# Hybrid block on one core: gates, attention output, GLU, merge and output projection with tokens on the partitions

## The chip, the cores and the metric

One core of a Trainium2 chip runs the whole kernel. Its engines are PE (matrix products and transposes), DVE and ACT (element work, conversions, copies), POOL (element work, a little of it here) and SP, whose queue issues the weight loads. Each runs its own instructions in order, and semaphores tie them together. The metric is the device time of one execution in microseconds; the median of three runs is given.

## The reference, cut to what matters

There are 256 tokens of width 1024, all in float32.

```python
h = rms_norm(x, norm_mix_g)
q, k, v, u, g = split(h @ w_in)              # 1024, 1024, 1024, 512, 2048 columns
o_a = attention(rotary(q), rotary(k), v)     # 8 heads of 128, causal, one block of 256
y   = gelu(ssm(u))                           # 512 channels
val, gt = split(y @ w_glu)                   # 1024 columns each
o_b = val * sigmoid(gt)
g_a, g_b = split(g)
mixed = sigmoid(g_a) * o_a + sigmoid(g_b) * o_b
x = x + mixed @ w_out
h = rms_norm(x, norm_mlp_g)
x = x + square(relu(h @ w_up)) @ w_down      # 4096 columns between
out = rms_norm(x, norm_final_g)
```

## The kernel before

Each float32 product is made of three products of parts: weights and activations are split into a high part in the format that PE takes at speed and a low part, and `mm3` (lines 85 to 88) issues high by high, high by low and low by high. Weights come in units of 128 partitions by 1024 numbers, 512 KB each. A unit is loaded by SP into one of five `raw` buffers, ACT casts it to `hi` (line 82), and DVE subtracts to get `lo` (line 83). There are four `hi` and four `lo` buffers, so a cast waits until PE has finished with the unit four before it.

Most projections keep channels on the partitions and tokens on the free axis: a 128x128 piece of the weights is stationary and 256 columns of activations stream against it. Values `v` (`v_chunk`) and the down projection have it the other way round: a 128x128 piece of the activations is stationary, 512 columns of weights stream, and the result has tokens on the partitions. The gates (`gate`) use `proj_pair`, two units at a time; the accumulated result is multiplied by the norm's factor `rs_bc`, laid along the free axis (line 317), and goes through a tanh on ACT. `attn_out` turns the probabilities on PE (`pt`, line 298), copies them out on ACT (`pts`, line 300), multiplies by `v` into `o`, and joins the gate `tha` to it. The GLU (lines 595 to 611) reads the SSM's output after a gelu, `yhl`, split in high and low, and merges with the second gate `thb` into `mxh` and `mxl`. The output projection (lines 618 to 633) adds the residual and leaves `x2h` and `x2l` for the up projection. `tok_major` (line 658) later turns the residual stream to token layout for the down projection.

The norm's factor per token is made by POOL in a short chain of small operations (`rsqrt`, lines 179 to 182) and then laid along the free axis by PE (`rs_ps`, line 196).

What comes after what is set in two steps. The string `ORDER` names the parts in program order: V the values, K a pair of heads' q and k, S scores and softmax, G and A the first gate and the attention output, B the second gate, Q and T the SSM, X a load of ACT's function table, Y the gelu. From the program order and the dependencies a scheduler then decides each engine's own order when the program is built. The splits of weights have a high priority there.

Of the kernel before, what the change touches and what calls it, by code (L numbers as in the profile page):

```python
# [13 lines left out]
ALU = mybir.AluOpType  # L14
# [29 lines left out]
ORDER = ("V0 V1 P0 T0 C0 Q0 T1 Q1 T2 K0 T3 X0 S0 G0 A0 G1 K1 K2 S1 Q2 A1 K3 G2 S2 A2 Q3 "  # L44
         "B0 B1 G3 S3 X1 Y0 A3 B2 B3")


def build(ctx, tc, dr, out):
# [151 lines left out]
    rs_bc = rs.unsqueeze(1).to_broadcast([P, 2, T])  # L200
# [42 lines left out]

    def v_chunk(c):
        acc = [mm_bank(f"v{c}{h}").rearrange("p a b -> p (a b)") for h in range(2)]
        for kk_ in range(4):
            wh, wl = in_unit(4 * c + kk_, "v")
            for k2 in range(2):
                k = 2 * kk_ + k2
                w2h, w2l = wh[:, k2 * 512 : (k2 + 1) * 512], wl[:, k2 * 512 : (k2 + 1) * 512]  # L250
                for hf in range(2):
                    xh, xl = xgh[:, k, hf * P : (hf + 1) * P], xgl[:, k, hf * P : (hf + 1) * P]
                    PE.matmul(acc[hf], xh, w2h, start=(k == 0), stop=False)
                    PE.matmul(acc[hf], xh, w2l, start=False, stop=False)
                    PE.matmul(acc[hf], xl, w2h, start=False, stop=(k == KD - 1))
# [15 lines left out]
    mixA = p1.tile([P, KD, T], F32, name="mixA")  # L271
# [31 lines left out]
    def attn_out(hp, prs, tha):  # L303
        pts = [attn_pt(x) for x in prs]
        o = att_bank("o")
        for j in range(2):
            hd = 2 * hp + j
            PE.matmul(o[:, j, :], v[:, 0, hd * P : (hd + 1) * P], pts[j][:, 0:256],
                      start=True, stop=False, skip_group_check=True)
            PE.matmul(o[:, j, 128:256], v[:, 1, hd * P : (hd + 1) * P], pts[j][:, 256:384],  # L310
                      start=False, stop=True, skip_group_check=True)
        V.scalar_tensor_tensor(mixA[:, 2 * hp : 2 * hp + 2, :], tha, 1.0, o,
                               op0=ALU.add, op1=ALU.mult)

    def gate(first, dst):
        acc = proj_pair(first, "g")
        V.tensor_mul(dst, acc, rs_bc)
        act(dst, dst, AF.Tanh, scale=0.5)

    def prepare():  # L320
# [82 lines left out]
        def cmul(o_r, o_i, x_r, x_i, y_r, y_i, neg_i):  # L403
            # (x_r + i x_i)(y_r + i y_i); with neg_i, x_i and o_i stand for minus their parts
# [146 lines left out]
    yhl = []  # L551

    def gelu():
        yhl.append(p1.tile([P, KD, T], F32R, tag="yhl", name="yhl"))
        yflat = yT.rearrange("p m e j -> p m (e j)")
        for m in range(4):
            act(yflat[:, m, :], yflat[:, m, :], AF.Gelu_apprx_tanh)
            split(yhl[0][:, m, :], yhl[0][:, 4 + m, :], yflat[:, m, :])

    thb, qk, prs, tha = [None] * 4, {}, {}, {}  # L560
    for step in ORDER.split():
# [12 lines left out]
        elif part == "K":  # L574
            qk[n] = (rope(proj_pair(8 + 6 * n, "q"), "q"), rope(proj_pair(10 + 6 * n, "k"), "k"))
# [3 lines left out]
        elif part == "G":  # L579
            tha[n] = p1.tile([P, 2, T], F32, tag="tha", bufs=2, name="tha")  # L580
            gate(12 + 6 * n, tha[n])
        elif part == "A":
            attn_out(n, prs.pop(n), tha.pop(n))
        elif part == "Y":
            gelu()
        elif part == "Q":
            ssm_quad(n)
        elif part == "B":
            thb[n] = p1.tile([P, 2, T], F32, tag=("cs", "sn")[n // 2], bufs=4, name=f"thb{n}")
            gate(32 + 2 * n, thb[n])  # L590

# [1 line left out]
    mxh = keep.tile([P, KD, T], F32R, tag="b40", name="mxh")  # L593
    mxl = keep.tile([P, KD, T], F32R, tag="b41", name="mxl")
    for m in range(KD):
        wh, wl = w_unit(dr["w_glu"][m], f"glu{m}")
        acc = mm_bank(f"glu{m}")
        for j in (1, 0):
            for k in range(4):
                o = (2 * k + j) * P  # L600
                mm3(acc[:, j, :], wh[:, o : o + P], wl[:, o : o + P],
                    yhl[0][:, k, :], yhl[0][:, 4 + k, :], k == 0, k == 3)
        sg = p1.tile([P, T], F32, tag="sg", bufs=2, name="sg")
        act(sg, acc[:, 1, :], AF.Tanh, scale=0.5)
        V.scalar_tensor_tensor(sg, sg, 1.0, acc[:, 0, :], op0=ALU.add, op1=ALU.mult)
        tb = thb[m // 2][:, m % 2, :]
        V.scalar_tensor_tensor(tb, tb, 1.0,
                               sg.rearrange("p (e j) -> p j e", e=2), op0=ALU.add, op1=ALU.mult)
        V.scalar_tensor_tensor(mixA[:, m, :], tb, 0.5, mixA[:, m, :],
                               op0=ALU.mult, op1=ALU.add)  # L610
        split(mxh[:, m, :], mxl[:, m, :], mixA[:, m, :])
    ph1.__exit__(None, None, None)

# [1 line left out]
    p2 = ctx.enter_context(tc.tile_pool(name="ph2", bufs=1))  # L615
    xT = p2.tile([P, KD, T], F32, name="xT2")
    nc.sync.dma_start(xT, dr["xT"])
    accs = [mm_bank(f"wo{i}") for i in range(3)] + [bank("y", 1, "wo3")]
    for k in range(KD):
        wh, wl = w_unit(dr["w_out"][k], f"wo{k}")  # L620
        for m in range(KD):
            mm3(accs[m // 2][:, m % 2, :], wh[:, m * P : (m + 1) * P], wl[:, m * P : (m + 1) * P],
                mxh[:, k, :], mxl[:, k, :], k == 0 and m % 2 == 0, k == KD - 1,
                skip_group_check=True)
    x2h = keep.tile([P, KD, T], F32R, tag="xh", name="x2h")
    x2l = keep.tile([P, KD, T], F32R, tag="xl", name="x2l")
    for i in range(4):
        xc = xT[:, 2 * i : 2 * i + 2, :]
        V.scalar_tensor_tensor(xc, accs[i], 0.5, xc, op0=ALU.mult, op1=ALU.add)  # L629
        for m in (2 * i, 2 * i + 1):  # L630
            S.activation(x2h[:, m, :], xT[:, m, :], AF.Copy, scale=g_mlp[:, m : m + 1])
            V.scalar_tensor_tensor(x2l[:, m, :], xT[:, m, :], g_mlp[:, m : m + 1],  # L632
                                   x2h[:, m, :].bitcast(F32), op0=ALU.mult, op1=ALU.subtract)

# [19 lines left out]
    x2t = p2.tile([P, 2, D], F32, name="x2t")  # L654
    sq2 = p2.tile([P, D], F32, name="sq2")
    st2 = p2.tile([P, 16], F32, name="st2")

    def tok_major():
        for hf in range(2):
            for c in range(2):  # L660
                tp = att_bank("tp").rearrange("p a b -> p (a b)")
                for i in range(4):
                    PE.transpose(tp[:, i * P : (i + 1) * P],
                                 xT[:, 4 * c + i, hf * P : (hf + 1) * P], ident)
                S.copy(x2t[:, hf, c * 512 : (c + 1) * 512], tp)
# [85 lines left out]
def _layout(inp):  # L751
# [16 lines left out]
    parts.append(seg["gb"].reshape(8, P, 1024))
# [61 lines left out]
```

## Time and profile before

| what | value |
|---|---|
| runs | 407.99, 406.92, 407.28 us; median 407.28 us |
| profiled execution | span 406.2 us; no other time of its own is given |
| PE busy | 395.7 us of the span (97%) |
| DVE busy | 295.0 us (73%) |
| ACT busy | 229.2 us (56%) |
| POOL busy | 33.8 us (8%) |
| DMA | 71.62 MB, mean 176 GB/s |

The span runs from the first to the last instruction that the profiler has of one execution. Matmuls overlap each other in the rows, so the distance between the starts of two neighbours, not the length of one, is what a matmul adds to PE's time. The granted clock of PE is given as a share of full speed; 1.00 is the level of 2.4 GHz and 0.50 that of 1.2 GHz.

### The profile page before, as it was taken

How to read it: one execution, taken by the hardware profiler on the slowest of the kernel's cores; microseconds unless marked ns; L12 is line 12 of the kernel's file. 1: busy time of each engine (PE TensorE's matmuls, PEld its weight loads, DVE VectorE, ACT ScalarE, POOL GpSimd, SP SyncE). 2: the span in 40 equal slices, each digit the busy share in tenths (PEclk: the TensorE clock that was granted, in tenths of full speed). 3: DMA queues.
4: the chain of work that ended last, by engine and by line, in shares of the span. 5: the costliest groups of instructions: out<-in, count | busy, mean ns of one | idle time of the engine just before them, and what ended most of it. 6: DMA issues, size and time to landing. Idle time of an engine off the chain costs nothing.

```text
span 406.2 us, 7401 instructions
## 1 busy us (share of the span) xinstructions
PE 395.7 (97%) x2907; PEld 369.5 (91%) x2907; DVE 295.0 (73%) x530; ACT 229.2 (56%) x363; POOL 33.8 (8%) x39
## 2 busy tenths in 40 slices
PE   7989999999999999999999999999999999999993
PEld 4968999999899998999999999999999888899983
DVE  6999899998998996769657656666666544563424
ACT  6878777464374565945637764545455344344323
POOL 4392562000000000000000000000000000000000
PEclk8999999999999999999999999999999999999998
DMA  7986843255526254366684365656565655565202
GB/s 223 390 326 189 264 146 99 89 188 171 162 63 207 73 163 141 111 195 215 186 330 160 119 215 185 194 171 197 169 197 168 203 194 181 195 207 166 94 0 105
DMA packets 22786, 71.62 MB, mean 176 GB/s; under 512 B 2784, under 2 KB 4832, under 8 KB 22624
## 3 DMA queue, kind: packets, MB, share of 16 engines
q1 hardware_dynamic: 20016, 69.18, 52.3%
q10 hardware_dynamic: 2736, 1.97, 1.6%
q8 instruction: 23, 0.38, 0.4%
q14 instruction: 11, 0.09, 0.1%
HBM read 69.18 MB, written 1.05 MB: 173 GB/s over the span
## 4 chain that ended last, share of the span: by engine, by line
PE 91%; DVE 3%; POOL 2%; issue 1%; DMA 1%; ACT 1%; SPq 0%; DVEq 0%
PE up L87 8%; PE up L86 8%; PE up L88 8%; PE dn L685 5%; PE dn L686 5%; PE dn L687 5%; PE g L86 4%; PE g L87 4%; PE g L88 4%; PE q L86 2%; PE k L87 2%; PE k L88 2%; PE q L87 2%; PE glu L88 2%; PE glu L87 2%; PE glu L86 2%
## 5 line engine op out<-in xcount | busy, mean ns | idle before, releaser
L86 PE MATMUL up<-x2h,hi_up 128*128 128x256 f32 x256 | 72.6, 284 | 0.1
L87 PE MATMUL up<-x2l,hi_up 128*128 128x256 f32 x256 | 72.7, 284 | 0.0
L88 PE MATMUL up<-x2h,lo_up 128*128 128x256 f32 x256 | 72.4, 283 | 0.0
L83 DVE TENSOR_TENSOR lo_dn<-raw_dn,hi_dn 128x1024 fp32r<-128x1024 f32 x32 | 39.2, 1226 | 43.4 <-ACT hi_dn L82 43.4
L82 ACT CAST hi_dn<-raw_dn 128x1024 fp32r<-128x1024 f32 x32 | 33.6, 1049 | 51.0 <-PE dn L687 24.7
L83 DVE TENSOR_TENSOR lo_up<-raw_up,hi_up 128x1024 fp32r<-128x1024 f32 x32 | 39.1, 1224 | 29.8 <-ACT hi_up L82 29.8
L82 ACT CAST hi_up<-raw_up 128x1024 fp32r<-128x1024 f32 x32 | 33.4, 1046 | 38.2 <-issue 17.9
L86 PEld LDWEIGHTS up<-x2h,hi_up 128*128 128x128 f32 x256 | 49.1, 192 | 0.3 <-DVE xT L629 0.3
L87 PEld LDWEIGHTS up<-x2l,hi_up 128*128 128x128 f32 x256 | 49.1, 192 | 0.2 <-DVE x2l L632 0.2
L88 PEld LDWEIGHTS up<-x2h,lo_up 128*128 128x128 f32 x256 | 49.1, 192 | 0.0
L686 PE MATMUL dn<-lo_dn,hh 128*128 128x512 f32 x96 | 37.5, 391 | 0.0
L685 PE MATMUL dn<-hi_dn,hh 128*128 128x512 f32 x96 | 37.5, 391 | 0.0
L687 PE MATMUL dn<-hi_dn,hl 128*128 128x512 f32 x96 | 37.4, 389 | 0.0
L87 PE MATMUL g<-xgl,hi_g 128*128 128x256 f32 x128 | 37.0, 289 | 0.0
L86 PE MATMUL g<-xgh,hi_g 128*128 128x256 f32 x128 | 37.0, 289 | 0.0
L88 PE MATMUL g<-xgh,lo_g 128*128 128x256 f32 x128 | 36.8, 288 | 0.0
L82 ACT CAST hi_g<-raw_g 128x1024 fp32r<-128x1024 f32 x16 | 16.8, 1047 | 20.9 <-PE q L87 7.4
L86 PEld LDWEIGHTS g<-xgh,hi_g 128*128 128x128 f32 x128 | 24.5, 191 | 0.4
L87 PEld LDWEIGHTS g<-xgl,hi_g 128*128 128x128 f32 x128 | 24.4, 191 | 0.3 <-issue 0.2
L88 PEld LDWEIGHTS g<-xgh,lo_g 128*128 128x128 f32 x128 | 24.5, 191 | 0.2
L687 PEld LDWEIGHTS dn<-hi_dn,hl 128*128 128x128 f32 x96 | 18.0, 188 | 3.8
L685 PEld LDWEIGHTS dn<-hi_dn,hh 128*128 128x128 f32 x96 | 18.1, 188 | 3.3
(258 smaller groups left out, 1104.6 us busy)
## 6 DMA issues: line engine op xcount, KB each, us to landing
raw_up<-w_up SPq DMA_DIRECT2D x32, 512.0 KB, 4.3
raw_dn<-w_down SPq DMA_DIRECT2D x32, 512.0 KB, 3.4
raw_g<-w_in SPq DMA_DIRECT2D x16, 512.0 KB, 3.9
raw_v<-w_in SPq DMA_DIRECT2D x8, 512.0 KB, 5.6
raw_q<-w_in SPq DMA_DIRECT2D x8, 512.0 KB, 3.8
raw_k<-w_in SPq DMA_DIRECT2D x8, 512.0 KB, 3.8
raw_glu<-w_glu SPq DMA_DIRECT2D x8, 512.0 KB, 3.4
raw_wo<-w_out SPq DMA_DIRECT2D x8, 512.0 KB, 3.6
```

The source lines that it names most:

```text
L82: S.copy(hi, x)
L83: V.tensor_sub(lo, x, hi.bitcast(F32))
L86: PE.matmul(o, wh, xh, start=first, stop=False, **kw)
L87: PE.matmul(o, wh, xl, start=False, stop=False, **kw)
L88: PE.matmul(o, wl, xh, start=False, stop=last, **kw)
L685: PE.matmul(acc, xh, wh[:, w], start=(k == 0), stop=False, skip_group_check=True)
L686: PE.matmul(acc, xh, wl[:, w], start=False, stop=False, skip_group_check=True)
L687: PE.matmul(acc, xl, wh[:, w], start=False, stop=(k == 31), skip_group_check=True)
```

## The change

Gates, attention output, GLU, merge, output projection and residual get tokens on the partitions. A pair of helpers, `tok_mm` and `tok_proj`, keeps a 128x128 piece of the activations stationary and streams 512 columns of weights. The host lays out the gates', GLU's and output projection's weights for it. A gate now covers 512 columns and four units, so there are four gates (G0, G1, B0, B1) where there were eight; the norm's factor is a number per partition in this layout and goes into the tanh as its scale, from a small new tile `rs_half`, so the multiplication by `rs_bc` is gone. The attention output has the turned probabilities stationary, in three matmuls of 128 columns per head where there were one of 256 and one of 128. The GLU goes in four quarters, and the merged result is turned back by 16 PE transposes (`mt`) and split out of PSUM. The output projection goes in two halves of 512 columns, adds the residual in token layout, and is turned back by 16 transposes (`xt`). The 16 transposes and four copies of `tok_major` and the second load of `xT` are gone; `x` is loaded in token layout instead.

```diff
-ORDER = ("V0 V1 P0 T0 C0 Q0 T1 Q1 T2 K0 T3 X0 S0 G0 A0 G1 K1 K2 S1 Q2 A1 K3 G2 S2 A2 Q3 "
-         "B0 B1 G3 S3 X1 Y0 A3 B2 B3")
+THA = 3
+ORDER = ("V0 V1 P0 T0 C0 Q0 T1 Q1 T2 K0 T3 X0 S0 G0 A0 K1 K2 S1 Q2 A1 K3 G1 S2 A2 Q3 "
+         "B0 S3 X1 Y0 A3 B1")
...
+    rs_half = p1.tile([P, 2], F32, name="rs_half")
     with tc.high_priority(RSP):
         rsqrt(G, rs_tok, rsm[:, 0:2], rsm[:, 4:6])
+    V.tensor_scalar(rs_half, rs_tok, 0.5, None, op0=ALU.mult)
...
+    def tok_mm(acc, wh, wl, xh, xl, k, hf, first, last):
+        rows = slice(hf * P, (hf + 1) * P)
+        PE.matmul(acc, xh[:, k, rows], wh, start=first, stop=False)
+        PE.matmul(acc, xh[:, k, rows], wl, start=False, stop=False)
+        PE.matmul(acc, xl[:, k, rows], wh, start=False, stop=last)
...
     def gate(first, dst):
-        acc = proj_pair(first, "g")
-        V.tensor_mul(dst, acc, rs_bc)
-        act(dst, dst, AF.Tanh, scale=0.5)
+        acc = tok_proj(first, "g")
+        for hf in range(2):
+            for i in range(2):
+                act(dst[i][:, hf, :], acc[hf][:, i * 256 : (i + 1) * 256], AF.Tanh,
+                    scale=rs_half[:, hf : hf + 1])
...
+    for q in range(4):
+        acc = wide_banks(f"glu{q}") if q % 2 else [flat(mm_bank(f"glu{q}{h}")) for h in range(2)]
+        for kk_ in range(2):
+            wh, wl = w_unit(dr["w_glu"][2 * q + kk_], f"glu{q}{kk_}")
+            for k2 in range(2):
+                k, w = 2 * kk_ + k2, slice(k2 * 512, (k2 + 1) * 512)
+                for hf in range(2):
+                    tok_mm(acc[hf], wh[:, w], wl[:, w], yhl[0][:, 0:4], yhl[0][:, 4:8], k, hf,
+                           k == 0, k == 3)
...
+            for i in range(2):
+                PE.transpose(tp[:, i, hf * P : (hf + 1) * P], ma[:, i * P : (i + 1) * P], ident)
+        split(mxh[:, 2 * q : 2 * q + 2, :], mxl[:, 2 * q : 2 * q + 2, :], tp)
...
-    def tok_major():
...
-                S.copy(x2t[:, hf, c * 512 : (c + 1) * 512], tp)
```

On DVE, in the middle of the values' projection, the order before is this. `lo_v` is a weight's low part, `s`, `q` and `tha` belong to the preparation of the SSM's tables there, and `rsm` holds the norm's factor that POOL is working on.

```order
L338 TENSOR_SCALAR s_551<-s_535 128x16
L350 SCALAR_TENSOR_TENSOR s_503<-s_501,s_495 128x16
L478 TENSOR_SCALAR tha<-q 128x512
L350 SCALAR_TENSOR_TENSOR s_539<-s_537,s_535 128x16
L350 SCALAR_TENSOR_TENSOR s_553<-s_551,s_535 128x16
```

And after:

```order
L351 TENSOR_SCALAR s_553<-s_537 128x16
L363 SCALAR_TENSOR_TENSOR s_505<-s_503,s_497 128x16
L491 TENSOR_SCALAR tha<-q 128x512
L196 TENSOR_SCALAR rs_half<-rsm 128x2
L363 SCALAR_TENSOR_TENSOR s_541<-s_539,s_537 128x16
L363 SCALAR_TENSOR_TENSOR s_555<-s_553,s_537 128x16
```

The new `rs_half`, which reads what POOL's chain leaves, stands in the middle of the tables' work; everything below it on DVE, the next `lo_v` among it, comes after it.

On ACT, where the last scores end and the GLU's input begins, the order before is this. `pr` are probabilities, `yT` the gelu in place, `pts` the turned probabilities, `hi_glu` a cast of a GLU weight, `yhl` the high part of the GLU's input.

```order
L105 ACTIVATE pr,st<-s,st 128x128
L105 ACTIVATE pr,st<-s,st 128x256
L82 CAST hi_glu_2260<-raw_glu_2258 128x1024
L99 ACT_TABLE_LOAD
L105 ACTIVATE yT<-yT 128x256 x3
L546 COPY yT<-y 32x128
L291 ACTIVATE pr<-pr,st 128x128
L292 ACTIVATE pr<-pr,st 128x256
L300 COPY pts<-pt 128x384
L82 CAST hi_glu_2298<-raw_glu_2296 128x1024
L82 CAST yhl<-yT 128x256
```

And after; `thb` are tanhs of the last gate, B1, and its casts `hi_glu` are now of 512 columns' layout:

```order
L106 ACTIVATE pr,st<-s,st 128x256
L100 ACT_TABLE_LOAD
L106 ACTIVATE yT<-yT 128x256 x4
L311 COPY pts<-pt 128x384
L106 ACTIVATE thb_1994<-g_1996,rs_half 128x256
L106 ACTIVATE thb_1995<-g_1996,rs_half 128x256
L302 ACTIVATE pr<-pr,st 128x128
L303 ACTIVATE pr<-pr,st 128x256
L83 CAST hi_glu_2152<-raw_glu_2150 128x1024
L106 ACTIVATE thb_1994<-g_1997,rs_half 128x256
L106 ACTIVATE thb_1995<-g_1997,rs_half 128x256
L83 CAST yhl<-yT 128x256 x4
```

Four tanhs have come in between the exponentials and the first `yhl`; the cast that stood behind the exponentials now stands just ahead of these rows.

On PE, at the start of the GLU, the order before is this: `g` are gate matmuls, `pt` the transposes of probabilities, `o` the attention output. Three more `g` follow these rows, and then the first `glu`.

```order
L298 MATMUL pt<-cst,pr 128x128 x2
L87 MATMUL g<-xgl,hi_g_2226 128x256
L88 MATMUL g<-xgh,lo_g_2227 128x256
L308 MATMUL o<-pts,v 128x256
L310 MATMUL o<-pts,v 128x128
L86 MATMUL g<-xgh,hi_g_2226 128x256
L87 MATMUL g<-xgl,hi_g_2226 128x256
L88 MATMUL g<-xgh,lo_g_2227 128x256
```

And after:

```order
L248 MATMUL g_1996<-hi_g_2054,xgh 128x512
L249 MATMUL g_1996<-lo_g_2055,xgh 128x512
L250 MATMUL g_1996<-hi_g_2054,xgl 128x512
L248 MATMUL g_1997<-hi_g_2054,xgh 128x512
L249 MATMUL g_1997<-lo_g_2055,xgh 128x512
L250 MATMUL g_1997<-hi_g_2054,xgl 128x512
L309 MATMUL pt<-cst,pr 128x128
L321 MATMUL o<-v,pts 128x128 x3
L309 MATMUL pt<-cst,pr 128x128 x2
L248 MATMUL glu_2076<-hi_glu_2080,yhl 128x512
```

The gate's matmuls now have 512 columns. Behind them stand one head's `pt` and `o`, the other head's `pt`, and then the GLU. Before, the last scores (`s`) stood 85 `g` matmuls ahead of the first `glu`. After, between the last matmul that reads the weight whose buffer the third GLU cast takes and the first `glu`, there are 12 `g` of 512 columns, six `pt` and three `o`.

## Rows read from the trace of the kernel before

**Rows 1.** Page, part 1: busy time and share of the span, number of instructions

```profile
PE 395.7 (97%) x2907; PEld 369.5 (91%) x2907; DVE 295.0 (73%) x530; ACT 229.2 (56%) x363; POOL 33.8 (8%) x39
```

**Rows 2.** Windows: from:to, us, busy (instructions) by engine, granted clock, DMA, GB/s

```profile
30.00:70.00 40.00, 40.00 (x273) 36.29 (x274) 38.17 (x82) 31.72 (x48) 16.98 (x15) 1.00 0.58 174
70.00:154.00 84.00, 84.00 (x708) 79.71 (x707) 80.35 (x147) 44.62 (x84) 0.00 (x0) 1.00 0.46 143
```

**Rows 3.** PE timeline in the up projection, first and last of 27 matmuls: start, us

```profile
254.78 0.28 PE L87 MATMUL up<-x2l,hi_up 128*128 128x256 f32 x1
...
257.90 0.28 PE L86 MATMUL up<-x2h,hi_up 128*128 128x256 f32 x1
```

**Rows 4.** PE timeline in the down projection, first and last of 19 matmuls

```profile
329.80 0.39 PE L686 MATMUL dn<-lo_dn,hh 128*128 128x512 f32 x1
...
333.88 0.39 PE L686 MATMUL dn<-lo_dn,hh 128*128 128x512 f32 x1
```

**Rows 5.** Lines by form: count, min/median/max ns, first and last start us

```profile
L86 PE MATMUL g<-xgh,hi_g x128: 278/283/385, 59.1 to 169.4; 128*128 128x256 f32 x128
```

**Rows 6.** PE timeline: transposes among gate matmuls

```profile
147.46 0.28 PE L87 MATMUL g<-xgl,hi_g 128*128 128x256 f32 x1
147.57 0.38 PE L298 MATMUL pt<-cst,pr 128*128 128x128 f32 x2
...
147.91 0.28 PE L86 MATMUL g<-xgh,hi_g 128*128 128x256 f32 x1
```

**Rows 7.** PE timeline at the start of the up projection

```profile
216.68 0.82 PE L86 MATMUL up<-x2h,hi_up 128*128 128x256 f32 x2
217.34 0.81 PE L663 MATMUL tp<-cst,xT 128*128 128x128 f32 x4
218.10 0.39 PE L87 MATMUL up<-x2l,hi_up 128*128 128x256 f32 x1
```

**Rows 8.** Timeline of all engines around the norm's rsqrt: start, us, idle before, releaser

```profile
22.10 0.24 POOL L180 TENSOR_TENSOR rsm<-rsm 128x2 f32<-128x2 f32 x1
...
22.37 1.22 DVE L83 TENSOR_TENSOR lo_v<-raw_v,hi_v 128x1024 fp32r<-128x1024 f32 x1
...
22.43 1.23 POOL L181 TENSOR_SCALAR rsm<-rsm 128x2 f32<-128x2 f32 x1
...
23.75 0.67 POOL L182 TENSOR_TENSOR rsm<-rsm 128x2 f32<-128x2 f32 x1
...
23.91 0.42 DVE L478 TENSOR_SCALAR tha<-q 128x512 f32<-128x512 f32 x1
...
27.67 1.21 DVE L83 TENSOR_TENSOR lo_v<-raw_v,hi_v 128x1024 fp32r<-128x1024 f32 x1
...
29.78 0.49 PE L196 MATMUL rs_ps<-cst,rsm 128*128 128x128 f32 x2 [1.55 <-POOL rsm L182]
```

**Rows 9.** ACT timeline from the last scores to the GLU's input

```profile
160.34 0.37 ACT L105 ACTIVATE pr<-s,st 128x128 f32<-128x128 f32 x1
...
162.21 1.28 ACT L99 ACT_TABLE_LOAD   x1
163.51 1.03 ACT L105 ACTIVATE yT<-yT 128x256 f32<-128x256 f32 x3
...
164.84 0.40 ACT L291 ACTIVATE pr<-pr,st 128x128 f32<-128x128 f32 x1
...
166.05 1.05 ACT L82 CAST hi_glu<-raw_glu 128x1024 fp32r<-128x1024 f32 x1
166.99 0.41 ACT L82 CAST yhl<-yT 128x256 fp32r<-128x256 f32 x1
```

**Rows 10.** PE timeline near the program's start

```profile
4.97 0.38 PE L86 MATMUL u_acc<-xgh,hi_u 128*128 128x256 f32 x1 [0.62 <-ACT hi_u L82]
...
6.42 0.39 PE L88 MATMUL u_acc<-xgh,lo_u 128*128 128x256 f32 x1 [0.62 <-DVE lo_u L83]
```

**Rows 11.** Windows: the stretch that followed

```profile
7.50:10.90 3.40, 3.38 (x16) 2.87 (x15) 2.85 (x9) 3.23 (x7) 0.00 (x0) 0.51 1.03 364
```

More of the change, by code (lines that the diff above doesn't have):

```diff
@@ L242, in build, with flat, tok_proj @@
     rsin_b = rsin.unsqueeze(1).to_broadcast([P, 2, T])
-    def v_chunk(c):
[L245 to L255, printed above, removed]
+    def tok_mm(acc, wh, wl, xh, xl, k, hf, first, last):
[3 more added lines that the diff above has]
+        PE.matmul(acc, xl[:, k, rows], wh, start=False, stop=last)
+    def flat(x):
+        return x.rearrange("p a b -> p (a b)")
+    def tok_proj(first, name):
+        acc = [flat(mm_bank(f"{name}{first}{h}")) for h in range(2)]
+        for kk_ in range(4):
+            wh, wl = in_unit(first + kk_, name)
+            for k2 in range(2):
+                k, w = 2 * kk_ + k2, slice(k2 * 512, (k2 + 1) * 512)
+                for hf in range(2):
+                    tok_mm(acc[hf], wh[:, w], wl[:, w], xgh, xgl, k, hf, k == 0, k == KD - 1)
+        return acc
+    def v_chunk(c):
+        acc = tok_proj(4 * c, "v")
         for hf in range(2):
@@ L306, in attn_out @@
         for j in range(2):
[L307 to L312, printed above, removed]
+            hd = slice((2 * hp + j) * P, (2 * hp + j + 1) * P)
+            cols = slice(j * P, (j + 1) * P)
+            for i, (t, first) in enumerate(((0, True), (1, False), (1, False))):
+                PE.matmul(o[:, t, cols], pts[j][:, i * P : (i + 1) * P], v[:, i // 2, hd],
+                          start=first, stop=(i != 1), skip_group_check=True)
+        V.scalar_tensor_tensor(mixA[:, :, hp * 256 : (hp + 1) * 256], tha, 1.0, o,
                                op0=ALU.add, op1=ALU.mult)
     def gate(first, dst):
-        acc = proj_pair(first, "g")
-        V.tensor_mul(dst, acc, rs_bc)
-        act(dst, dst, AF.Tanh, scale=0.5)
+        acc = tok_proj(first, "g")
[3 more added lines that the diff above has]
+                    scale=rs_half[:, hf : hf + 1])
     def prepare():
@@ L557, in gelu @@
             act(yflat[:, m, :], yflat[:, m, :], AF.Gelu_apprx_tanh)
-            split(yhl[0][:, m, :], yhl[0][:, 4 + m, :], yflat[:, m, :])
+            y_ = yT[:, m].rearrange("p e j -> p j e")
+            yh, yl = (yhl[0][:, 4 * i + m, :].rearrange("p (j e) -> p j e", e=2) for i in range(2))
+            split(yh, yl, y_)
     thb, qk, prs, tha = [None] * 4, {}, {}, {}
@@ L579, in build @@
         elif part == "G":
-            tha[n] = p1.tile([P, 2, T], F32, tag="tha", bufs=2, name="tha")
-            gate(12 + 6 * n, tha[n])
+            for i in range(2):
+                tha[2 * n + i] = p1.tile([P, 2, T], F32, tag="tha", bufs=THA, name="tha")
+            gate(24 + 4 * n, [tha[2 * n + i] for i in range(2)])
         elif part == "A":
@@ L588, in build @@
         elif part == "B":
-            thb[n] = p1.tile([P, 2, T], F32, tag=("cs", "sn")[n // 2], bufs=4, name=f"thb{n}")
-            gate(32 + 2 * n, thb[n])
+            for i in range(2):
+                thb[2 * n + i] = p1.tile([P, 2, T], F32, tag=("cs", "sn")[n], bufs=4,
+                                         name=f"thb{2 * n + i}")
+            gate(32 + 4 * n, [thb[2 * n + i] for i in range(2)])
     mxh = keep.tile([P, KD, T], F32R, tag="b40", name="mxh")
     mxl = keep.tile([P, KD, T], F32R, tag="b41", name="mxl")
[L595 to L611, printed above, removed]
@@ L612, in build @@
     ph1.__exit__(None, None, None)
     p2 = ctx.enter_context(tc.tile_pool(name="ph2", bufs=1))
[L616 to L624, printed above, removed]
+    x2t = p2.tile([P, 2, D], F32, name="x2t")
@@ L633, in build @@
                                    x2h[:, m, :].bitcast(F32), op0=ALU.mult, op1=ALU.subtract)
+    for hf in range(2):
+        S.activation(sq2, x2t[:, hf, :], AF.Square, accum_out=st2[:, hf : hf + 1])
+    V.tensor_scalar(st2[:, 2:4], st2[:, 0:2], 1.0 / D, EPS, op0=ALU.mult, op1=ALU.add)
+    V.reciprocal(st2[:, 4:6], st2[:, 2:4])
     hh = p2.tile([P, FF // P, T], F32R, name="hh")
```

84 lines of the change are left out of this document (50 added, 34 removed).

## The prediction, made before the changed kernel ran

> **What bounds the kernel now.** I read the page's busy shares first. PE is busy 97% of the span, the next engine 73% [rows 1]. Then a table of windows: between 70 and 154 us, where most of the gates lie, PE is busy for all of 84 us at full clock, with DVE at 80 of 84 [rows 2]. So PE sets the time there, and DVE or ACT count only where PE would have to stop for them. Dropping the gates' multiplication from DVE is therefore worth nothing by itself. What the change can win is PE time, and what it can lose is a new stop of PE. I looked for stops in PE's timeline and found two that the change touches: 1.55 us ahead of `rs_ps` [rows 8] and a slow start of the up projection [rows 7].
>
> **The streaming.** Twenty-six intervals of 256-column matmuls take 257.90 - 254.78 = 3.12 us, 0.120 us each [rows 3]. Eighteen of 512 columns take 4.08 us, 0.2267 us each [rows 4]. Two narrow ones cost 0.240 us and one wide one 0.2267 us, a saving of 13.3 ns a pair. The gates have 3 times 128 narrow matmuls [rows 5]; the GLU and the output projection have 192 each by the code's loops (8 units of 24). That is 768 narrow ones, 384 pairs: **-5.1 us**. Both spacings come from stretches like the ones that change, with PE never waiting, so I take the value with little doubt.
>
> The Trainium skill speaks against this term: on its page "TensorE: Matmul & The Clock Gate" (Part 1) a streaming matmul costs its columns at 2.4 GHz and then only about 2.5 ns more. An estimate by that page is 2.6 ns a pair and 1.0 us in all; this trace differs, with 13.3 ns a pair.
>
> **The transposes.** From 147.46 to 147.91 us PE takes two matmuls of 256 columns and two transposes [rows 6]: 0.45 - 0.24 = 0.21, so 0.105 us a transpose. The change adds 16 `mt` and 16 `xt` and removes 16 `tp`, net 16: **+1.7 us**. They read what DVE has just written. The last `mt` stands ahead of the output projection and the last `xt` ahead of the up projection; I looked there in the new PE order and found other matmuls between enough for the work of DVE and ACT, so no wait is added.
>
> The attention output streams 384 columns per head as before, in three matmuls for two. A matmul of 128 columns is near the 0.105 us of a transpose, so a head is between 0 and 0.1 us dearer, at most 0.8 us for eight; the wider one gets cheaper by its half, and I take 0.
>
> **The start of the up projection.** From 216.68 to 218.10 us PE issues two `up` and four `tp`, 1.42 us [rows 7], where 2 x 0.12 + 4 x 0.105 = 0.66 would do. The new order has the second half's transposes behind matmuls of the first half's channels, so **-0.7 us**; bounds 0 and -0.8.
>
> **The small `rs_half`.** It stands on DVE behind a `tha` operation that ended at 23.91 + 0.42 = 24.33 us [rows 8], and it reads the end of POOL's chain, which PE saw at 29.78 us. DVE takes instructions in order, so it stops there, with the tables' work, and each later `lo_v`, queued behind it. But POOL would then go faster. In the rows a POOL operation on 128x2 numbers that ran beside a long DVE operation ended just after it: 22.43 + 1.23 = 23.66 against 22.37 + 1.22 = 23.59, and 23.75 + 0.67 = 24.42 against 24.33. Where none was beside it, it took 0.24 us and the next started 0.33 us after its start [rows 8]. Eight of these operations are left at 24.42: with DVE standing still they end at 24.42 + 8 x 0.33 = 27.1. DVE is then 27.1 - 24.3 = 2.8 us late. PE's stop of 1.55 us for `rs_ps` goes. The `lo_v` of 27.67 was done at 28.88, 0.9 us ahead of PE's restart at 29.78; that lead swallows 0.9 of the 2.8, and 1.9 reach PE. Net **+0.3 us**. Bounds: -1.55 if DVE catches up unseen, +1.25 if all 2.8 reach PE.
>
> **The gap ahead of the GLU.** This is the term that decides. The first GLU matmul needs `yhl`, the last step of a long row on ACT that begins at the exponentials of the last scores. Before, PE had 85 gate matmuls, 10 us, between the last scores and the GLU. After, a gate is one block of four units, and most of the last one stands ahead of these scores. The cast of the third GLU weight waits for the buffer of the gate's last unit but one; on ACT it stands ahead of the exponentials. From that point ACT has to do, with durations of [rows 9]: the cast and two exponentials (162.21 - 160.34) 1.87; the table load (163.51 - 162.21) 1.30; four gelus at 1.03 / 3 = 0.35, 1.40; four tanhs of the same shape, 1.40; two scalings and the copy `pts` (166.05 - 164.84) 1.21; another cast (166.99 - 166.05) 0.94; one `yhl` 0.41. The sum is 8.5 us. PE has in that time 12 x 0.2267 + 6 x 0.105 + 3 x 0.105 = 3.7 us of work, and the second head's transposes in it wait for ACT too. So PE stands still for 8.5 - 3.7 = **4.8 us**. Bounds: 0 if the GLU's input were ready in time after all (PE elsewhere late by as much), and 6 if DVE's maxima and low parts stand in the row as well. I take 4.8, since each duration has a row of the same shape.
>
> **The clock in that gap.** Between 4.97 and 6.42 us PE had three matmuls with waits of 0.62 us between them [rows 10]; from 7.5 to 10.9 us the granted clock was 0.51 [rows 11], the level of 1.2 GHz, though PE was busy then. The wait of 1.55 us at 28 us brought nothing of the kind: the window from 30 to 70 us has 1.00 [rows 2]. A gap of 4.8 us, broken only by a few transposes, is nearer to the first. Half clock for 3.4 us of full work costs 1.7 us; some of it may fall within the gap itself. I take **+1.3 us**, bounds 0 and 1.7.
>
> **Sum.** -5.1 + 1.7 - 0.7 + 0.3 + 4.8 + 1.3 = +2.3 us on the span of 406.2, so 408.5. The median of the runs, 407.28, is 1.1 us above that span; with the same 1.1 the time is **409.6 us**.
>
> **The rivals.**
> - *The gap without the clock's fall.* The few transposes and `o` matmuls keep the clock up, as the short wait at 28 us did. -1.3: **408.3 us**.
> - *The gap is filled and the streaming arrives (faster).* One mechanism: PE reaches the last gate units 5 us later relative to ACT than I reckon, because ACT has run ahead; the third GLU cast finds its buffer free early and the ACT row is over when PE gets to the GLU. It decides from the point where the cast no longer waits for the gate's unit. Then neither 4.8 nor 1.3 is paid: **403.5 us**. For it: ACT is busy only 56% [rows 1]. Against it: a buffer can't come free before PE has read it, and the row begins there.
> - *POOL keeps its old end.* If the slow POOL operations had another cause than DVE, `rs_half` still waits until 29.7; DVE is late by 5.4 us instead of 2.8, and 2.6 more reach PE: **412.2 us**. For it: one POOL operation, or its gap, may be slow for itself. Against it: the ends that agree in the rows to 0.1 us.
> - *Wide matmuls win nothing*, as they would if a matmul cost PE its columns alone: two narrow ones then take as long as a wide one, and the streaming is worth 0 and not 5.1. The time is 409.6 + 5.1 = **414.7 us**. Against it: 26 and 18 intervals in this very kernel. The Trainium skill, on "TensorE: Matmul & The Clock Gate" (Part 1), comes near to this rival; this trace differs, as above.
>
> **Chances.** Forecast 0.40; gap without the clock's fall 0.22; filled gap 0.18; POOL's old end 0.10; no gain from streaming 0.04; another late wait, somewhere I haven't seen, 0.06. A measurement of this kernel tells 0.3% from no change, that is 1.2 us: faster is below 406.06, slower above 408.50. Faster takes the filled gap and a little of a halved gap: 0.20. Same is mostly the gap without the clock's fall, and some of the forecast with a smaller gap: 0.26. Slower is the rest: 0.54. The range goes from 404.8, between the filled gap and the half-filled one, to 412.4, just above POOL's old end; left out are most of the filled gap and the wide-matmul case. The forecast's own range is 408.4 to 411.
>
> **What would show it.** In the profile of the changed kernel: wide gate, GLU and output matmuls 0.227 us apart; POOL's chain over near 27 us, with DVE idle on POOL before it and no wait at `rs_ps`; some stop of PE for `lo_v` behind it; one gap of PE ahead of the first GLU matmul, 4 to 6 us, with ACT as what it waits for and a table load in it; a granted clock near 0.5 behind it; no stop at the up projection's start. The forecast is wrong if the gap is under 3 us, if the clock stays at 1.00 behind it, or if PE waits on POOL's chain by more than 2 us net.

## The result and the profile after

The changed kernel takes 410.23 us (median of 4 runs, 409.16 to 411.61) against 407.48 us for the kernel before beside it: a ratio of 1.0067, 95% interval 1.0044 to 1.009. Its profiled execution has a span of 408.5 us, 2.3 us more than before. PE was still the bound; from part 1 of the page of the changed kernel (busy us, share of the span, instructions):

```profile
PE 394.7 (97%) x2555; PEld 350.9 (86%) x2555; DVE 291.5 (71%) x519; ACT 226.7 (56%) x363; POOL 33.2 (8%) x39
```

PE has 352 instructions fewer than before [rows 1], and is busy 1.0 us less. The list of what PE waited for (us in total, times, longest) has two waits that the kernel before did not have, both ahead of the GLU, one new one among the values, and none for POOL any more:

```profile
PE pt L309 <- ACT pr L302: 3.0, 1, 3.0
...
PE glu L248 <- ACT yhl L83: 1.2, 1, 1.2
PE v L249 <- DVE lo_v L84: 0.9, 1, 0.9
```

Where the two lie, in PE's timeline of the changed kernel; the last gate matmul is the first row:

```profile
165.46 0.39 PE L250 MATMUL g<-hi_g,xgl 128*128 128x512 f32 x1
168.84 0.33 PE L309 MATMUL pt<-cst,pr 128*128 128x128 f32 x1 [2.99 <-ACT pr L302]
...
169.67 0.38 PE L309 MATMUL pt<-cst,pr 128*128 128x128 f32 x2
171.26 0.80 PE L248 MATMUL glu<-hi_glu,yhl 128*128 128x512 f32 x1 [1.20 <-ACT yhl L83]
171.85 0.63 PE L249 MATMUL glu<-lo_glu,yhl 128*128 128x512 f32 x1
172.27 0.63 PE L248 MATMUL glu<-hi_glu,yhl 128*128 128x512 f32 x1
...
174.50 0.40 PE L248 MATMUL glu<-hi_glu,yhl 128*128 128x512 f32 x1
174.74 0.39 PE L249 MATMUL glu<-lo_glu,yhl 128*128 128x512 f32 x1
```

PE has nothing from 165.46 + 0.39 to 168.84 us, then one head's attention output and the other head's transposes, and nothing again until 171.26. From 171.85 the GLU's matmuls of 512 columns come 0.43 us apart, and from 174.50 on 0.24 and less. The window says the same of the clock (columns as in [rows 2]):

```profile
171.00:174.50 3.50, 3.24 (x8) 2.61 (x9) 1.76 (x5) 1.68 (x5) 0.00 (x0) 0.56 0.44 150
```

What PE waits for is ACT's row, which the prediction added up from [rows 9]. After the change, in ACT's timeline:

```profile
162.76 1.05 ACT L83 CAST hi_glu<-raw_glu 128x1024 fp32r<-128x1024 f32 x1 [1.81 <-PE g L250]
163.84 0.37 ACT L106 ACTIVATE pr<-s,st 128x128 f32<-128x128 f32 x1
...
164.77 1.28 ACT L100 ACT_TABLE_LOAD   x1
166.06 1.33 ACT L106 ACTIVATE yT<-yT 128x256 f32<-128x256 f32 x4
167.30 0.46 ACT L311 COPY pts<-pt 128x384 f32<-128x384 f32 x1
167.66 0.84 ACT L106 ACTIVATE thb<-g,rs_half 128x256 f32<-128x256 f32 x2
168.38 0.40 ACT L302 ACTIVATE pr<-pr,st 128x128 f32<-128x128 f32 x1
...
169.07 1.04 ACT L83 CAST hi_glu<-raw_glu 128x1024 fp32r<-128x1024 f32 x1
170.01 0.85 ACT L106 ACTIVATE thb<-g,rs_half 128x256 f32<-128x256 f32 x2
170.73 1.57 ACT L83 CAST yhl<-yT 128x256 fp32r<-128x256 f32 x4
```

The cast of a GLU weight waited 1.81 us for the gate's buffer and started at 162.76; the exponentials, the table load, the gelus, a copy, two tanhs and two scalings follow; the next transposes wait for the scaling of L302, over at 168.78, and start at 168.84. Then a cast, two more tanhs, and the first `yhl` at 170.73. From 162.76 to the first GLU matmul are 8.50 us; the prediction had 8.5.

At the other place, DVE and POOL around the small tile (timeline of all engines, changed kernel):

```profile
24.37 0.41 DVE L491 TENSOR_SCALAR tha<-q 128x512 f32<-128x512 f32 x1
...
24.50 0.34 POOL L180 TENSOR_TENSOR rsm<-rsm 128x2 f32<-128x2 f32 x1
...
26.62 0.19 POOL L183 TENSOR_TENSOR rsm<-rsm 128x2 f32<-128x2 f32 x1
...
26.85 0.17 DVE L196 TENSOR_SCALAR rs_half<-rsm 128x2 f32<-128x2 f32 x1 [2.06 <-POOL rsm L183]
```

DVE is idle for 2.06 us, POOL's eight operations take 24.50 to 26.81 us, and PE's 1.55 us for `rs_ps` [rows 8] are gone.

By stretches, from the starts of PE's first and last matmuls of a kind (us):

| stretch | before | after | short row | filler |
|---|---|---|---|---|
| start to the last `u_acc` | 20.90 | 21.28 | 21.14 | 20.19 |
| to the last `v` | 23.79 | 22.89 | 22.89 | 23.18 |
| to the first `glu` | 125.11 | 127.09 | 123.32 | 127.10 |
| to the last `wo` | 46.62 | 48.49 | 47.07 | 47.15 |
| first to last `up` | 94.38 | 92.90 | 92.90 | 92.90 |
| first to last `dn` | 88.50 | 88.91 | 88.91 | 88.91 |

The last two columns are runs of the next section. After less before: +0.38, -0.90, +1.98, +1.87, -1.48, +0.41, in all the 2.3 us; what lies between the stretches and at the end makes under 0.1.

### The profile page after: what moved, and what is told of

The parts are those of the page before. It is cut to its first block, busy times and chain, and to the rows that moved or that the text cites. A ratio compares the mean times of both kernels' runs of the same rounds, so it can differ in the third digit from the quotient of the medians.

```text
span 408.5 us, 6697 instructions
## 1 busy us (share of the span) xinstructions
PE 394.7 (97%) x2555; PEld 350.9 (86%) x2555; DVE 291.5 (71%) x519; ACT 226.7 (56%) x363; POOL 33.2 (8%) x39
## 3 DMA queue, kind: packets, MB, share of 16 engines
q10 hardware_dynamic: 2736, 1.97, 1.6%
## 4 chain that ended last, share of the span: by engine, by line
PE 87%; DVE 4%; ACT 3%; DMA 2%; issue 1%; POOL 1%; SPq 1%; DVEq 0%; ACTq 0%
PE up L88 8%; PE up L89 8%; PE up L87 8%; PE dn L708 5%; PE dn L707 5%; PE dn L706 5%; PE g L248 3%; PE g L250 3%; PE g L249 3%; PE glu L248 2%; PE glu L249 2%; PE q L89 2%; PE k L88 2%; PE k L89 2%; PE k L87 2%; PE q L88 2%
## 5 line engine op out<-in xcount | busy, mean ns | idle before, releaser
L248 PE MATMUL g<-hi_g,xgh 128*128 128x512 f32 x64 | 25.5, 401 | 0.0
L249 PE MATMUL g<-lo_g,xgh 128*128 128x512 f32 x64 | 25.4, 397 | 0.0
L250 PE MATMUL g<-hi_g,xgl 128*128 128x512 f32 x64 | 25.3, 395 | 0.0
L707 PEld LDWEIGHTS dn<-lo_dn,hh 128*128 128x128 f32 x96 | 18.0, 188 | 3.6
L84 DVE TENSOR_TENSOR lo_g<-raw_g,hi_g 128x1024 fp32r<-128x1024 f32 x16 | 19.6, 1223 | 1.8 <-ACT hi_g L83 1.8
L88 PE MATMUL k<-xgl,hi_k 128*128 128x256 f32 x64 | 18.5, 290 | 0.0
```

The lines of the kernel that those rows point to most:

```text
L84: V.tensor_sub(lo, x, hi.bitcast(F32))
L88: PE.matmul(o, wh, xl, start=False, stop=False, **kw)
L248: PE.matmul(acc, xh[:, k, rows], wh, start=first, stop=False)
L249: PE.matmul(acc, xh[:, k, rows], wl, start=False, stop=False)
L250: PE.matmul(acc, xl[:, k, rows], wh, start=False, stop=last)
L707: PE.matmul(acc, xh, wl[:, w], start=False, stop=False, skip_group_check=True)
```

## The experiments

The theory is that of the prediction: the change saves PE time, and ACT's row ahead of the GLU, with the clock behind it, takes back more. The row is the chain of ACT instructions from the cast to the first `yhl`; filler is work that PE has in its order while it would otherwise wait for that chain. The rivals: the stop is a symptom and only moves when it is taken away; the clock falls for another reason; wide matmuls win nothing; the small tile is what costs. Ratios are to the kernel before, run beside each.

**e1, the short row.**

```diff
-            gate(32 + 4 * n, [thb[2 * n + i] for i in range(2)])
+            gate(32 + 4 * n, [thb[2 * n + i] for i in range(2)], ycast if n else ())
...
-            wh, wl = w_unit(dr["w_glu"][2 * q + kk_], f"glu{q}{kk_}")
+            wh, wl = w_unit(dr["w_glu"][2 * q + kk_], f"glu{q}{kk_}", after=ycast if q else ())
...
+            V.tensor_scalar(pr[:, 0:128], pr[:, 0:128], st[:, 4:5], None, op0=ALU.mult)
+            V.tensor_scalar(pr[:, 128:384], pr[:, 128:384], st[:, 5:6], None, op0=ALU.mult)
...
-        acc = wide_banks(f"glu{q}") if q % 2 else [flat(mm_bank(f"glu{q}{h}")) for h in range(2)]
+        acc = wide_banks(f"glu{q}") if q % 2 == 0 else [flat(mm_bank(f"glu{q}{h}")) for h in range(2)]
```

Here `ycast` are the casts of the GLU's input, and `after` orders an ACT instruction behind them; the scalings on DVE are for the last pair of heads alone.

> The changed kernel with ACT's row ahead of the GLU shortened: the casts of the GLU weights from the third on and the last gate's tanhs are ordered behind the casts of the GLU's input, the scalings of the last probabilities go from ACT to DVE, and the first GLU quarter takes the wide PSUM banks so that it does not need the gate's. PE's order ahead of the GLU stays. If the two stops of PE there (2.99 and 1.20 us) and the clock behind them (about 1.6 us) are what makes the change slower, PE's stops fall under 1 us, the GLU's first matmuls come about 0.23 us apart, and the time is 404.5 to 405.5 us, 0.6% below the kernel before. The rival is that the stop only moves, to the GLU's low parts, the probabilities or the merge: then 409 to 410 us with another wait in PE's list.

Measured: 404.63 us, ratio 0.9926 (0.9907 to 0.9946). Of PE's waits behind 30 us these are left:

```profile
PE v L250 <- DVE lo_v L84: 0.9, 1, 0.9
PE o L326 <- ACT pts L316: 0.6, 1, 0.6
```

The clock behind it, by a window:

```profile
168.00:176.00 8.00, 8.00 (x40) 6.68 (x39) 6.09 (x7) 6.08 (x11) 0.00 (x0) 1.00 0.42 139
```

So the stop did not move: without it the same change is 5.6 us faster than as it was made, and 3.1 us faster than the kernel before.

**e2, the filler.**

```diff
+            if n == 1:
+                fill = flat(bank("y", 1, "fill"))
+                for _ in range(12):
+                    PE.matmul(fill, xgh[:, 0, 0:P], flat(xgh[:, 0:2, :]), start=True, stop=True)
```

> The changed kernel with 12 needless matmuls of 512 columns behind the last gate, into a PSUM bank that nobody reads, so that PE works through the longer stop of 2.99 us. They add no time if they fit. If the clock fell because PE stood still there, it stays at 1.00 and the first GLU matmuls come 0.23 us apart instead of 0.43: 1.6 us less than the changed kernel, 408.6 us. If the fall has another cause, the first GLU matmuls stay at 0.43 and the time at 410.2 us.

Measured: 408.34 us, ratio 1.0021 (1.0011 to 1.0032). PE's timeline:

```profile
164.89 2.88 PE L612 MATMUL fill<-xgh 128*128 128x512 f32 x12
168.05 0.33 PE L309 MATMUL pt<-cst,pr 128*128 128x128 f32 x1 [0.27 <-ACT pr L302]
...
170.47 0.50 PE L248 MATMUL glu<-hi_glu,yhl 128*128 128x512 f32 x1 [1.20 <-ACT yhl L83]
170.80 0.39 PE L249 MATMUL glu<-lo_glu,yhl 128*128 128x512 f32 x1
171.03 0.40 PE L248 MATMUL glu<-hi_glu,yhl 128*128 128x512 f32 x1
```

The second stop of 1.20 us is as it was, and the GLU's matmuls now come 0.23 us apart from the second on: with PE at work in the 2.99 us, the clock stays. From the first `glu` to the last `wo` 47.15 us against 48.49, and 49.02 in a second profile of the changed kernel (e12): the clock's fall cost 1.34 and 1.87 us there. The times differ by 1.9 us (410.23 - 408.34). The spans of the two profiles differ by 2.2 us, but 0.8 of that lies ahead of the last `v`, which the filler does not touch.

**e3, narrow streams.**

```diff
+        for xx, ww, f, l in ((xh, wh, first, False), (xh, wl, False, False), (xl, wh, False, last)):
+            for c in range(2):
+                cc = slice(c * 256, (c + 1) * 256)
+                PE.matmul(acc[:, cc], xx[:, k, rows], ww[:, cc], start=f and c == 0, stop=l,
+                          skip_group_check=True)
```

> The kernel of the short row, but each wide matmul of the gates, GLU and output projection is issued as two of 256 columns with the same stationary piece (768 for 384; the values stay wide). By the forecast's 13.3 ns a pair it is 5.1 us slower than the short row, about 410 us; by the 0.230 us that the changed kernel shows for a wide matmul, 10 ns a pair, 3.8 us slower, about 408.7 us. If streaming 512 columns wins nothing, it equals the short row, about 405 us.

Measured: 409.78 us, ratio 1.0055 (1.0037 to 1.0073), 5.15 us above e1, as the 13.3 ns would have it. But the trace shows that not all of it is streaming. PE's list has a wait that e1 has not:

```profile
PE xt L677 <- DVE x2t L675: 1.7, 1, 1.7
```

By stretches e3 has 1.27 us more than e1 from the last `v` to the first `glu`, and 4.02 more from there to the first `up`. Taking out the 1.7 us of that wait, and adding the 0.6 us that e1 alone waits at `o`, leaves 4.2 us for 384 pairs, 10.9 ns each. This is an estimate: it takes each wait at its whole length, and the scheduler's order is not the same (84 narrow gate matmuls behind the last scores in e3, the work of 42 wide ones, where e1 has 19). That wide matmuls win nothing is refuted; the forecast's 13.3 ns were, by this estimate, somewhat too much.

**e4, the output projection alone**: of the change, only the hunks of the output projection, the residual, `tok_major` and the layout of `w_out`, applied to the kernel before.

```diff
-            mm3(accs[m // 2][:, m % 2, :], wh[:, m * P : (m + 1) * P], wl[:, m * P : (m + 1) * P],
...
+                for hf in range(2):
+                    tok_mm(acc[hf], wh[:, w], wl[:, w], mxh, mxl, k, hf, k == 0, k == KD - 1)
...
-        if i == 2:
-            tok_major()
```

> The kernel before with the output projection and the residual alone taken from the change: 96 wide matmuls for 192 narrow ones, 16 transposes for 16, no first gate, GLU or attention output changed. By the terms: streaming -1.0 to -1.3 us, transposes 0, start of the up projection -0.7 us, so 1.7 to 2.0 us below the kernel before, about 405.6 us, with no stop of PE at 216 us. The rival is that the transposes between the halves wait for DVE's residual or ACT's scalings: then PE's list shows a wait there and the time is 407 us or more.

Measured: 405.59 us, ratio 0.9956 (0.9939 to 0.9974), and no wait of PE at the residual. Its stretches, though, are 0.42 us less than before from `glu` to `wo`, 1.49 less in `up`, and 1.83 less in the values, which this edit does not touch. The expected time came out, and a good part of it for another reason; e10 and e11 come back to it.

**e5 and e6, the row's parts one by one**: of the diff of e1, e5 has the line of `w_unit` alone, e6 those of `gate` and `acc`.

> The changed kernel with one part of the short row alone: the casts of the GLU weights from the third on are ordered behind the casts of the GLU's input. The cast ahead of the exponentials waited until 162.76 us for the gate's weight buffer and held them until 163.84; without it they can start when DVE has the maxima, about 162.0. That and the second cast take 2.8 us out of ACT's row. If the row sets the stop, PE's stops ahead of the GLU fall from 4.19 us to about 1.4, none of them as long as the 2.99 us that the clock fell behind, and the time is about 405.8 us. If the casts are not what holds the row, the stops stay near 4 us and the time at 410 us.

Measured: 406.01 us, ratio 0.9968 (0.9956 to 0.9981). PE's waits at the GLU, and a window behind them:

```profile
PE pt L310 <- ACT pr L303: 1.6, 1, 1.6
...
PE glu L249 <- ACT yhl L83: 0.3, 1, 0.3
```

```profile
170.00:174.00 4.00, 4.00 (x19) 3.30 (x19) 3.48 (x5) 3.45 (x6) 0.00 (x0) 1.00 0.19 37
```

1.9 us of stops for 4.19, and the clock stays up. So the two casts in the row, the first of which waits for the gate's weight buffer, make over half of the stops.

> The other part alone: the last gate's four tanhs behind the casts of the GLU's input (and the first GLU quarter in the wide PSUM banks). It takes 1.6 us of tanhs out of ACT's row, half of it ahead of the last probabilities' scalings. If the row sets the stop, PE's stops fall from 4.19 to about 2.6 us; the first is then about 2.3 us, between the 1.55 us that the clock stayed up behind in the kernel before and the 2.99 us that it fell behind here. The time is 408.6 us if the clock falls all the same and 407.0 us if it stays up. If the tanhs only ran in time that was idle anyway, 410 us.

Measured: 410.81 us, ratio 1.0093 (1.0077 to 1.0108).

```profile
PE pt L310 <- ACT pr L303: 2.3, 1, 2.3
...
PE xt L664 <- DVE x2l L669: 1.1, 1, 1.1
...
PE wo L250 <- DVE lo_wo L84: 0.8, 1, 0.8
```

The stop at the GLU is the 2.3 us that the row gave, and the clock fell behind it (0.50 from 169 to 171 us). The time is 2.2 us above the 408.6 all the same: the scheduler put the transposes of the first half of the output projection four matmuls ahead of the up projection, and PE waits there for DVE and ACT, and for a low part of `wo`. These waits come to 2.3 us. They belong to this kernel's order and not to the tanhs: e1 moves the tanhs too, has 12 matmuls at that place, and waits for none of the three.

**e7, the kernel before with the small tile**, whose result nothing reads.

```diff
         rsqrt(G, rs_tok, rsm[:, 0:2], rsm[:, 4:6])
+    rs_half = p1.tile([P, 2], F32, name="rs_half")
+    V.tensor_scalar(rs_half, rs_tok, 0.5, None, op0=ALU.mult)
```

> The kernel before with the small tile for half the norm's factor made by DVE at the place where the change has it, read by nobody: DVE stands there until POOL's chain is over. The forecast had this at +0.3 us net, bounds -1.55 and +1.25. The trace of the changed kernel shows POOL's chain over at 26.8 us, no wait of PE for it, and 0.9 us of PE for a late low part; read from the end of the SSM's input matmuls to the end of the values, 22.9 us against 23.8 us before, the stand is a gain of 0.9 us. If that is so here, this stretch is 22.9 us and the time 406.8 us or less; if the stand costs, the stretch is over 23.8 us and the time over 407.7 us.

Measured: 407.7 us, ratio 1.001 (1.0001 to 1.0019). POOL's chain is over at 26.05 us, and the stretch to the last `v` is 22.25 us, less than was expected, against 23.79 before; but the scheduler also left 66 gate matmuls instead of 85 ahead of the GLU, and there PE's list has 0.9 us of waits that it had not. The stand itself is a gain in the trace, and the time does not show it.

**e8, the short row with the small tile late.**

```diff
-    V.tensor_scalar(rs_half, rs_tok, 0.5, None, op0=ALU.mult)
...
-    V.tensor_mul(rsin, sin_c, rs)
+    sin_in = V.tensor_mul(rsin, sin_c, rs).ins
+    behind(V.tensor_scalar(rs_half, rs_tok, 0.5, None, op0=ALU.mult).ins, [sin_in])
```

> The kernel of the short row, but DVE makes half the norm's factor only behind the rotary tables, when POOL has long been done, so it does not stand for it. In the stretch from the SSM's input matmuls to the values' end, POOL's chain should then end near 29 us again, with a wait of PE of up to 1.5 us for it, and without the 0.9 us for the late low part; the stretch is 23.5 to 24 us if the stand helps and about 22 us if it costs. The scheduler also puts all gate matmuls ahead of the last scores here, so nothing fills PE's time between them and the GLU: by the row on ACT (two exponentials, table load, gelus, one copy and cast, about 5 us, less the transposes and the attention output) a stop of 4 us there again, with the clock's fall, some 5 us on top of 404.6 us.

Measured: 412.1 us, ratio 1.0127 (1.0101 to 1.0154), 2.5 us more than expected. The stretch to the last `v` is 21.96 us, and PE did not wait for POOL, whose chain was over at 26.36 us and not near 29: the late tile was better here. Between the last scores and the GLU PE waited 2.8 us for probabilities and 0.4 for `yhl`, and half clock followed. With that, 130.30 us to the first `glu` against 123.32 in e1; some 2 of these 7 us lie ahead of the last gate matmul, and which order makes them was not tried.

**e9 and e10, the short row in another order of the parts**, without and with the late tile of e8.

```diff
-         "B0 S3 X1 Y0 A3 B1")
+         "S3 X1 Y0 A3 B0 B1")
```

> The kernel of the short row with the last scores and the gelu named ahead of both second gates in the order of the parts, so that 24 wide gate matmuls stand between the last scores and the GLU, among the transposes and the attention output, and no gate matmul's buffer is waited for. The stop of 0.6 us that the short row still had for the copied probabilities should go: 404.0 us against its 404.6. If something else than the row at the GLU holds it, the same 404.6.

Measured: 415.17 us, ratio 1.0181 (1.0165 to 1.0197), a clear miss. PE's timeline:

```profile
160.58 0.49 PE L314 MATMUL pt<-cst,pr 128*128 128x128 f32 x3
162.21 0.61 PE L314 MATMUL pt<-cst,pr 128*128 128x128 f32 x3 [1.14 <-DVE pr L304]
164.90 1.65 PE L326 MATMUL o<-v,pts 128*128 128x128 f32 x6 [2.08 <-ACT pts L316]
166.20 0.77 PE L249 MATMUL g<-hi_g,xgh 128*128 128x512 f32 x1
166.78 0.63 PE L250 MATMUL g<-lo_g,xgh 128*128 128x512 f32 x1
```

There is enough filler, but it stands behind the waiting instructions: PE takes `pt` and `o` in its order, waits 1.14 and 2.08 us for them, and the gate matmuls come after. From the second on those are 0.43 us apart. In `up` there is a wait for `xt` of 1.4 us, at the place of e6's 1.1, and behind it half clock once more, 0.50 from 224.8 to 228.2 us.

> The same order of the parts, and DVE makes half the norm's factor only behind the rotary tables. The stretch from the SSM's input matmuls to the values' end was 22.0 us in two kernels where DVE did not stand for POOL and 22.9 to 23.3 us in those where it did, so 0.9 us less than the run beside it: 403.1 us. If the stand is worth nothing or helps, 404 us or more.

Measured: 418.48 us, ratio 1.0252 (1.0222 to 1.0282). The stretch to the last `v` is 25.79 us, not 22. The timeline of all engines:

```profile
27.36 1.94 POOL L182 TENSOR_TENSOR rsm<-rsm 128x2 f32<-128x2 f32 x1
27.42 0.68 DVE L498 SCALAR_TENSOR_TENSOR tha<-tha,q 128x512 f32<-128x512 f32 x1
...
28.02 1.21 DVE L84 TENSOR_TENSOR lo_v<-raw_v,hi_v 128x1024 fp32r<-128x1024 f32 x1
...
30.47 0.38 PE L199 MATMUL rs_ps<-cst,rsm 128*128 128x128 f32 x1 [1.97 <-POOL rsm L184]
```

A POOL operation of 128x2 numbers lies beside two DVE operations and takes 1.94 us; PE waits 1.97 for the chain, and from 31.0 to 34.4 us the granted clock is 0.50.

**e11 and e12, both kernels again**, for a second profile (408.0 and 410.9 us, one run each).

> The kernel before, unchanged, for a second profile. If the stop of 1.55 us for POOL's chain belongs to this kernel, it is there again and the stretch to the values' end is 23.8 us; if it belonged to that one execution, the stretch is 22 us, as in the run with the output projection alone, whose code is the same up to there.

```profile
26.87 1.94 POOL L180 TENSOR_TENSOR rsm<-rsm 128x2 f32<-128x2 f32 x1
...
29.64 0.49 PE L196 MATMUL rs_ps<-cst,rsm 128*128 128x128 f32 x2 [1.63 <-POOL rsm L182]
```

The wait is there again, 1.63 us, with the same POOL operation of 1.94; the stretch is 23.89. Both profiles of this kernel have it, so it was not one odd execution. Yet e4, whose DVE and POOL have the same order there, had none, and its POOL chain was over at 26.97. In e4 DVE waited 0.51 us for a cast before an earlier `lo_v`; the `lo_v` of this place began 0.6 us later, and POOL had passed. One thing was not there again: from 7.5 to 10.9 us the granted clock is 1.00 in this profile, where [rows 11] have 0.51.

> The changed kernel, unchanged, for a second profile. The two stops ahead of the GLU, 2.99 and 1.20 us, and the half clock behind them are there again within 0.1 us, since nothing in that row depends on how the execution began; the stretch to the values' end is again 22.8 to 23.3 us.

```profile
168.95 0.48 PE L309 MATMUL pt<-cst,pr 128*128 128x128 f32 x1 [2.99 <-ACT pr L302]
169.21 1.49 PE L321 MATMUL o<-v,pts 128*128 128x128 f32 x6
...
171.36 0.79 PE L248 MATMUL glu<-hi_glu,yhl 128*128 128x512 f32 x1 [0.23 <-ACT yhl L83]
```

The first stop is 2.99 us again. The second is 0.23 and not 1.20, since the clock had fallen by the transposes already and `pt` and `o` took longer; the first GLU matmul starts at 171.36, 0.1 us from the first profile. The stretch to the last `v` is 23.24.

## Why the prediction was right, step by step

The time came out at 410.23 for 409.6 and the span at 408.5 for 408.5. Term by term:

- **What bounds it.** PE did, and the two new stops decided the sign; e1 shows that the kernel is 0.74% faster than before without them. The rival of the filled gap fails at the point where it decides: the cast still waited, 1.81 us, for the gate's unit.
- **Streaming, -5.1.** The sign was right and the size too large, by the estimate from e3 against e1, 4.2 us. In the GLU of the changed kernel 15 intervals do give 0.2267 us, the spacing of [rows 4]:

```profile
181.38 0.39 PE L250 MATMUL glu<-hi_glu,yhl 128*128 128x512 f32 x1
...
184.78 0.39 PE L250 MATMUL glu<-hi_glu,yhl 128*128 128x512 f32 x1
```

  but among the gates, between other matmuls, rows lie 0.23 us apart. And the saving is no constant of the two shapes. In the down projection of the changed kernel, whose code is the same as before, the 288 wide matmuls lie 0.233 us apart in the mean and its 192 narrow ones 0.114, where the kernel before has 0.228 and 0.119: there two narrow ones cost 0.228, less than a wide one. By the Trainium skill's 2.5 ns above the columns (page "TensorE: Matmul & The Clock Gate", Part 1) an estimate of the term is 1.0 us; e3 speaks against it.
- **Transposes, +1.7, and the start of the up projection, -0.7.** Right together: `up` is 1.48 us shorter, which is the 0.7 and eight transposes net (16 out, eight in) at about 0.1. The other 24 new ones lie from `glu` to `wo`, where e2, whose clock did not fall, has 0.53 us more than before; 24 at 0.108 less 192 pairs at 10.9 ns would be 0.5. No wait stands at the new ones; eight in a row:

```profile
216.32 1.03 PE L662 MATMUL xt<-cst,x2t 128*128 128x128 f32 x8
```

- **The small tile, +0.3.** The steps came as forecast: DVE stood 2.06 us for the 2.8 estimated, POOL's chain was over at 26.81 for 27.1, the stop for `rs_ps` went, and a low part came late. The net did not, and the term is a gain: only 0.88 us of the lateness reached PE for 1.9, and the stretch is 0.90 us shorter (23.24 against 23.89 in the second profiles, 0.65). "POOL keeps its old end" is refuted. But the chain was also early in e4 and e8, where DVE does not stand for it, so the 29.7 that the term started from was not a fixed end.
- **The gap, +4.8.** Not one gap of 4 to 6 us but two stops, 2.99 and 1.20, together 4.19 us, with PE's transposes and `o` between them. Taken singly, the longer one is at the 3 us under which the prediction called itself wrong; what the sum needs is the total. ACT's row was as long as added up, 8.5 us. PE had 4.3 us of work beside it and not 3.7: the three `o` of the order stand as six rows in the trace, some 0.3 us more, and the rest lies in the ends of the last matmul before each stop, which the spacing leaves out.
- **The clock, +1.3.** 1.34 us by stretches in the first profile of the changed kernel and 1.87 in the second (against e2). That the clock fell because PE stood still is shown by e2. The likeness that the forecast drew, to the fall near the program's start [rows 11], is weaker than it looked: the same kernel's second profile has 1.00 there (e11).
- **Not in the sum:** the start up to the last `u_acc`, +0.38, which also differs between executions of one kernel (20.68 in e11, 20.90 before); and the down projection, whose code is the same, at 88.91 us for 88.50 in every kernel with the new output projection. Its wide matmuls take 1.4 us more and its narrow ones 1.0 less; the cause stays open.

With what was measured the sum is -4.2 + 1.7 - 0.7 - 0.9 + 4.2 + 1.3 + 0.8 = +2.2 us, of 2.3. Against the forecast the streaming was off by +0.9, the small tile by -1.2, the gap by -0.6, and +0.8 was not in the sum. So it is luck that the total came within 0.1 us; that the two stops and the clock outweigh the streaming is not.

## What to carry to other kernels

When a change makes the bound engine's work shorter, count the filler that it leaves between the last input of a serial row on another engine and the first use of that row's result; the row keeps its length. Adding the row up from a profile's durations, and the filler from the order, gave the stop to 0.6 us before anything ran. A stop of the bound engine can cost more than its length, as the half clock behind it shows; and an order that looks better by the count of filler (e9) is worse if the filler stands behind what waits.

## What the runs showed of the hardware

- The granted clock, and what PE did before it fell: behind single stops of 1.55 us [rows 8], 1.63 us (e11), 1.6 us (e5) and 1.7 us (e3) it was 1.00; behind the stops of 1.97 us (e10), 2.3 us (e6) and 2.99 us (changed kernel, twice) it fell to 0.50, the level of 1.2 GHz, at which the GLU's matmuls stand 0.43 us apart. The length of a stop does not settle it alone: behind the same two stops at the start of the up projection, 0.25 and 1.38 us, the clock fell to 0.50 in e9 and stayed at 1.00 in e10.
- A POOL operation on 128x2 numbers takes 0.2 us alone and up to 1.94 us beside DVE's long ones, and where it falls is a matter of half a microsecond in when a cast is over: the same order of DVE and POOL had its chain end at 29.73 and 29.59 us (before, twice) and at 26.97 (e4); with the late tile it ended at 26.36 (e8) and 30.42 (e10). With DVE standing for it, it ended between 25.96 and 26.86 us in nine profiles, which is the steadier place. The Trainium skill ("SBUF — State Buffer", Terms) says that DVE and GpSimd (POOL) share a pair of SBUF ports under an exclusive lock held for the full instruction, and that the loser fully blocks. The rows of e10 agree: the POOL operation of 1.94 us is over at 29.30, just behind the second of the two DVE operations beside it, at 29.23.
